# Attention operands written twice over into DRAM in full-width form, loads cut in pieces, bias copied per head

## The chip, the cores and the metric

The kernel runs on one core of a Trainium2 chip, as one program with one launch. The metric is the device time of that program in microseconds. All DMAs of the kernel are issued by SyncE (SP), on one queue that feeds the core's 16 DMA engines.

## The reference

One inference step of a hybrid decoder layer, in float32, for a prompt of 2048 tokens and 64 sample tokens (8 sequences of 8). The width is 1024; eight attention heads of 64 take one half of it and eight RWKV-7 heads of 64 the other.

```
def decoder_layer(x, k_past, v_past, wkv0, shift0, bias_table, ...):
    n = rms_norm(x, ln1_g)
    proj = n @ w_in                       # 1024 -> 1536 (q, k, v) + 1824 (RWKV)
    q = head_rms(q, q_norm_g);  k = head_rms(k, k_norm_g)
    att = dilated_attention(q, k_ctx, v_ctx, ...)
    rw, wkv_T, shift_T = rwkv7_time_mix(proj[..., 1536:], ...)
    h = x + concat(att, rw) @ w_out
    return h + square(relu(rms_norm(h, ln2_g) @ w_mlp1)) @ w_mlp2

# dilated_attention, for each (window, dilation) of (128, 1), (512, 4), (2048, 16):
s = einsum(q, k) * scale + bias[bucket(distance)];  e = exp(s - max);  o = e @ v
# the three branch outputs are merged, weighted by their denominators
```

The bias depends on head and distance alone: 32 buckets, 8 heads.

## The kernel before, in words

Float32 products are made from two-part operands: a tensor is split into a rounded high part and the rest, and each product is three matmuls (high x high, high x low, low x high).

The program has three stages. In the first (to about 1209 us) the projections run in four groups of 512 tokens (`proj`, `rproj`, `qkv`), and between their matmuls stand those of the RWKV recurrence, nine units one after the other (`core`). In the second (to about 1640 us) attention runs over four pairs of heads (`attention`), and the sample tokens' attention and the output projection follow. The third, from about 1960 us, is the MLP. The order of the instructions on each engine is laid down when the program is built, by a scheduler that plays a timeline; an instruction goes where its operands are ready in that timeline, by priority. On each engine the order is then fixed. Of the DMAs on SP the same holds: an issue that waits holds up all behind it. Eight semaphores serve the DMAs in turn, so that an issue also waits for the DMA eight places before it.

Weights come in panels of 256 KB (`wpanel`, L313): loaded to `wr`, of which there are two, then split by ACT and DVE into `wh` and `wl`, of which there are four each.

`qkv` makes q, k and v for a group. For q and k, `transposed_out` (L818) transposes two heads of a pair at a time, and writes a high part `qhi` and a low part `qlo` of 128 x 512 to DRAM (L831, L832), one DMA each, into `qhD`, `qlD`, `khD` and `klD`, which are laid out [pair, 128, 2048]. For k a third tile `ko` goes to an output. All of these, and others, share three buffers (tag `xg`). Group 0's q, k and v come last, after the last unit's projections.

`bias_vectors` (L458) makes, in group 1, the bias by distance for three branches (`bv1`, 8 heads x 1152), from one-hot tables `oh` by a matmul with the bias table (L468); it then copies `bv1` from DRAM to DRAM, 128 rows alike per head, into `bvD` (L477): two DMAs of four heads each. Seven more such one-hot pieces follow for the sample tokens. The generator is stepped once per `rproj` of group 1.

`attention(p)` needs for each of the pair's two heads three tiles of 128 x 2048: `kst` (high part of k in the upper and again in the lower 64 partitions), `klo` (the low part of k, twice) and `qst` (high part of q above, low part below). One matmul over 128 partitions then gives the sum of two products. `kq_load` (L994) loads them with twelve DMAs of 64 partitions, 512 KB each. Pair p+1's loads are written where branch 1 of pair p begins; two sets of tiles alternate, so pair 2's wait until pair 0 has ended. A pair takes 20 steps, in groups that each need a tile of V (`vt`, L1023, four buffers). While pair p+1 runs, the merge of pair p is stepped between its steps (`merge`): its weights go out to DRAM (`wD`, L1166), come back as rows (`wrow`, L1169), and a matmul spreads them over the partitions (`ax`, L1176).

Of the kernel before, what the change touches and what calls it, by code (L numbers as in the profile page):

```python
# [170 lines left out]
def _build(ctx, tc, nc, I, O, dbg, upto):  # L171
# [39 lines left out]
    qhD = dram.tile([4, P, T], F32, name="qhD")  # L211
    qlD = dram.tile([4, P, T], F32, name="qlD")
    khD = dram.tile([4, P, T], F32, name="khD")
    klD = dram.tile([4, P, T], F32, name="klD")
# [243 lines left out]
    def bias_vectors():  # L458

        btab = c1.tile([33, 8], F32, name="btab")  # L460
        nc.sync.dma_start(out=btab, in_=I["btab"])
        bv1 = dram.tile([8, 3, 384], F32, name="bv1")

        def by_distance(src, n):
            oh = wp.tile([P, 512], F32, name="oh", tag="qn", bufs=3)
            nc.sync.dma_start(out=oh[:33, :n], in_=src)
            ps = pj()
            PE.matmul(ps[:8, :n], btab, oh[:33, :n], start=True, stop=True)  # L468
            sb = wp.tile([P, 512], F32, name="sb", tag="qn", bufs=3)
            act(sb[:8, :n], ps[:8, :n], AF.Copy)  # L470
            return sb

        for b in range(3):
            nc.sync.dma_start(out=bv1[:, b], in_=by_distance(I["oneh"][:, b], 384)[:8, :384])
            yield
        for h in range(0, 8, 4):
            nc.sync.dma_start(out=bvD[h:h + 4].rearrange("h p b n -> h p (b n)"), in_=bc(bv1[h:h + 4].rearrange("h b n -> h (b n)"), 1, P))  # L477
        for c in range(0, NSV, 512):
            n = min(512, NSV - c)
            nc.sync.dma_start(out=svD[:, :, c:c + n], in_=bc(by_distance(I["soneh"][:, c:c + n], n)[:8, :n], 1, 8))  # L480
            yield
# [214 lines left out]
    def proj(g, nh, nl):  # L696

        other = qkv(g, nh, nl) if g else iter(())
        for i, j in enumerate((12, 13, 14, 4, 0, 8, 5, 1, 9, 6, 2, 10, 7, 3, 11)):
            rproj(g, j, nh, nl)  # L700
            if g == 1:
                next(bias, None)
# [68 lines left out]
    def qkv(g, nh, nl):  # L771
# [46 lines left out]
        def transposed_out(cp, qn):  # L818
            isq = cp < 2
            gg = gq if isq else gk  # L820
            hD, lD = (qhD, qlD) if isq else (khD, klD)
            h0 = (cp % 2) * 2
            for pp in range(2):
# [7 lines left out]
                nc.sync.dma_start(out=hD[h0 + pp, :, gs], in_=hi.bitcast(F32))  # L831
                nc.sync.dma_start(out=lD[h0 + pp, :, gs], in_=lo.bitcast(F32))  # L832
# [161 lines left out]
    def kq_load(p):  # L994

        kq = kqs[p % 2]
        K = []
        for ty in range(2):
            rr = slice(ty * 64, ty * 64 + 64)
            kst = kq.tile([P, T], F32R, name=f"kst{ty}", tag="kq")  # L1000
            klo = kq.tile([P, T], F32R, name=f"klo{ty}", tag="kq")
            qst = kq.tile([P, T], F32R, name=f"qst{ty}", tag="kq")
            for dst, src, r0 in ((kst, khD, 0), (qst, qhD, 0), (kst, khD, 64), (qst, qlD, 64), (klo, klD, 0), (klo, klD, 64)):
                nc.sync.dma_start(out=dst[r0:r0 + 64].bitcast(F32), in_=src[p, rr])
            K.append((kst, klo, qst))
        return K

# [29 lines left out]
    def attention(p, pump, ahead):  # L1037

        K = ahead.pop(("kq", p))
        st = at.tile([P, 2, 3, 4, 2, 4], F32, name="st", bufs=2)  # L1040
        ob = [at.tile([P, T], F32, name=f"ob{b}", bufs=2 if b == 0 else 1) for b in range(3)]
        for b in range(3):
            bts = ahead.pop(("bias", p, b))
            if p < 3:
                if b == 1:
                    ahead["kq", p + 1] = kq_load(p + 1)
                if b:
                    ahead["bias", p + 1, b - 1] = bias_load(p + 1, b - 1)
            vt = None
            for grp in range(4):  # L1050
                vp, vt = vt, next_v()
                o = ppo.tile([P, 512], F32, name="o")
                for t2 in range(0, 4, 2 if b < 2 else 4):
# [38 lines left out]
                    pump()  # L1092
                if b == 0:
# [3 lines left out]
                else:  # L1097
                    act(ob[b].rearrange("p (m r) -> p m r", r=16)[:, :, grp * 4:(grp + 1) * 4], o.rearrange("p (r m) -> p m r", r=4), AF.Copy)
        if p < 3:
# [83 lines left out]
    ahead = {("kq", 0): kq_load(0)}  # L1183
    for b in range(3):
        ahead["bias", 0, b] = bias_load(0, b)
    vq.append(next(vgen))
# [179 lines left out]
    for nm, t in (("mixR", mixR), ("mixA", mixA), ("qhD", qhD), ("qlD", qlD), ("khD", khD), ("klD", klD)):  # L1366
# [180 lines left out]
```

## Time and profile before

| | |
|---|---|
| median of 3 runs | 3410.0 us (3407.44 to 3411.9) |
| profiled execution, whole program | 3415.77 us |
| its span, first to last instruction | 3414.0 us |
| TensorE busy | 3209.2 us, 94% |
| VectorE, ScalarE, GpSimd busy | 50%, 39%, 12% |
| DMA | 364.73 MB, mean 107 GB/s |

Busy shares are averages over stages that have different limits, so the profile is read by stretch: which engine is busy there, and what the others wait for. PE is TensorE, DVE VectorE, ACT ScalarE, POOL GpSimd, and SPq the queue on which SyncE issues DMAs. The DMA share is the mean over the 16 DMA engines of the time in which they move packets, and GB/s is what they moved. A DMA's row on SPq shows its issue, not its transfer; a long one is an issue that was held up.

### The profile page before, as it was taken

The numbers are of one execution on the slowest core, as the hardware profiler recorded it, in microseconds if no ns is written. First come the engines' busy times: TensorE is split into PE (matmuls) and PEld (weight loads), VectorE is DVE, ScalarE is ACT, GpSimd is POOL, SyncE is SP. The second block draws the span as 40 slices with busy tenths as digits, with TensorE's granted clock in tenths as the row PEclk, the third lists the DMA queues.
The fourth block names the chain that finished last, engine by engine and source line by source line (L and its number), as shares of the span: only waits on it lengthen the run. The fifth ranks groups of instructions, "written<-read, shape, count | busy, mean of one in ns | idle before, by whom it ended". The sixth has DMA issues, their size and how long they took to land.

```text
span 3414.0 us, 60201 instructions
## 1 busy us (share of the span) xinstructions
PE 3209.2 (94%) x23646; PEld 2791.4 (82%) x23646; DVE 1713.4 (50%) x3951; ACT 1326.7 (39%) x3209; POOL 395.2 (12%) x713
## 2 busy tenths in 40 slices
PE   5959999999999979989899999999999999999999
PEld 5836877786788857878688899999999988888887
DVE  4635676677677525546554643333333633333333
ACT  4435564565455536657322322222222322222221
POOL 1003243342354100111000000000000000000000
PEclk9979999999999989999899999999999999999999
DMA  5445464465355495333776111111111211111112
GB/s 165 136 141 161 131 191 139 119 174 145 112 146 153 131 212 113 94 87 99 261 244 206 44 47 44 47 44 44 44 46 44 97 49 49 48 50 47 50 47 74
DMA packets 336968, 364.73 MB, mean 107 GB/s; under 512 B 112907, under 2 KB 226374, under 8 KB 333612
## 3 DMA queue, kind: packets, MB, share of 16 engines
q1 hardware_dynamic: 336684, 360.88, 36.5%
q8 instruction: 186, 3.05, 0.4%
q14 instruction: 98, 0.80, 0.1%
HBM read 286.20 MB, written 79.30 MB: 107 GB/s over the span
## 4 chain that ended last, share of the span: by engine, by line
PE 59%; DMA 6%; DVE 2%; SPq 1%; issue 1%; ACT 1%; POOL 1%; DVEq 0%; ACTq 0%; POOLq 0%
PE pm L1505 21%; PE pm L1488 21%; PE pwo L1431 4%; PE o L1091 2%; PE sc L1066 2%; PE pt L1084 2%; PE sc L1067 2%; PE pj L789 1%; DMA kst<-khD 1%; DMA vt<-vD 1%; DMA kv<-in_kc 1%; DMA mr<-mixA 1%; SPq L1421 1%; PE sc L1233 0%; DMA wD<-wh 0%
## 5 line engine op out<-in xcount | busy, mean ns | idle before, releaser
L184 ACT ACTIVATE wh<-wr 128x512 fp32r<-128x512 f32 (+1 forms) x472 | 294.3, 624 | 1027.5 <-PE pm L1505 582.3
L181 DVE TENSOR_TENSOR wl<-wr,wh 128x512 fp32r<-128x512 f32 (+1 forms) x472 | 325.9, 692 | 425.0 <-ACT wh L184 410.7
L1488 PE MATMUL pm<-mml,wh 128*128 128x512 f32 (+2 forms) x1280 | 452.5, 354 | 3.3 <-DVE mml L181 3.3
L1488 PE MATMUL pm<-mmh,wh 128*128 128x512 f32 (+2 forms) x1280 | 454.8, 356 | 0.4 <-ACT mmh L184 0.4
L1488 PE MATMUL pm<-mmh,wl 128*128 128x512 f32 (+2 forms) x1280 | 452.8, 354 | 0.0
L1505 PE MATMUL pm<-fh,wh 128*128 128x512 f32 (+2 forms) x1280 | 450.5, 355 | 0.0
L1505 PE MATMUL pm<-fh,wl 128*128 128x512 f32 (+2 forms) x1280 | 449.6, 353 | 0.0
L1505 PE MATMUL pm<-fl,wh 128*128 128x512 f32 (+2 forms) x1280 | 448.4, 352 | 0.0
L181 DVE TENSOR_TENSOR h<-pm,h 128x364 f32<-128x364 f32 (+1 forms) x320 | 190.5, 598 | 423.9 <-PE pm L1505 423.7
L1488 PEld LDWEIGHTS pm<-mml,wh 128*128 128x128 f32 x1280 | 241.0, 188 | 27.4 <-DVE mml L181 5.9
L1488 PEld LDWEIGHTS pm<-mmh,wl 128*128 128x128 f32 x1280 | 241.9, 189 | 22.5
L1505 PEld LDWEIGHTS pm<-fh,wl 128*128 128x128 f32 x1280 | 240.7, 188 | 22.4
L1488 PEld LDWEIGHTS pm<-mmh,wh 128*128 128x128 f32 x1280 | 241.4, 189 | 19.9 <-ACT mmh L184 0.9
L1505 PEld LDWEIGHTS pm<-fl,wh 128*128 128x128 f32 x1280 | 240.0, 188 | 21.5
L1505 PEld LDWEIGHTS pm<-fh,wh 128*128 128x128 f32 x1280 | 240.3, 188 | 19.2
L789 PE MATMUL pj<-wh,nh 128*128 128x256 f32 (+1 forms) x816 | 237.3, 292 | 7.5 <-ACT qn L184 3.5
L789 PE MATMUL pj<-wh,nl 128*128 128x256 f32 (+1 forms) x816 | 236.2, 290 | 1.0 <-DVE nl L181 0.9
L330 PE MATMUL pj<-nh,wh 128*128 128x512 f32 (+3 forms) x600 | 222.7, 375 | 13.2 <-ACT nh L184 9.9
L789 PE MATMUL pj<-wl,nh 128*128 128x256 f32 (+1 forms) x816 | 234.6, 288 | 0.0
L330 PE MATMUL pj<-nl,wh 128*128 128x512 f32 (+3 forms) x600 | 221.6, 370 | 3.9 <-DVE nl L181 3.8
L330 PE MATMUL pj<-nh,wl 128*128 128x512 f32 (+3 forms) x600 | 217.5, 365 | 0.0
L184 ACT ACTIVATE e<-e,st 128x256 f32<-128x256 f32 (+1 forms) x384 | 174.3, 455 | 106.3 <-DVE st L1069 104.4
(295 smaller groups left out, 6105.3 us busy)
## 6 DMA issues: line engine op xcount, KB each, us to landing
wr<-in_w SPq DMA_DIRECT2D x256, 256.0 KB
wr<-in_wr SPq DMA_DIRECT2D x120, 256.0 KB
wr<-in_wq SPq DMA_DIRECT2D x96, 256.0 KB
kv<-in_kc SPq DMA_DIRECT2D x40, 512.0 KB
kv<-in_vc SPq DMA_DIRECT2D x40, 512.0 KB
xsD<-xst SPq DMA_DIRECT2D x56, 256.0 KB
xrkv<-xsD SPq DMA_DIRECT2D x32, 384.0 KB
vt<-vD SPq DMA_DIRECT2D x48, 256.0 KB
```

The source lines that it names most:

```text
L181: V.tensor_tensor(out, a, b, op)
L184: S.activation(out, in_, func, bias=bias, scale=scale, **kw)
L330: PE.matmul(ps[:m, :n], a[:, k, :m], b[h * 4 + k][:, c0:c0 + n], start=(h == 0 and i == 0), stop=(h == 1 and i == 11))
L789: PE.matmul(out, a[h * 2 + k][:, i * P:i * P + m], b[:, k, :], start=(h == 0 and q == 0 and i % 2 == 0), stop=(h == 3 and q == 5 and (i % ...
L1066: PE.matmul(ps[:, c0:c0 + n], cols(qst, b, i, False), cols(kst, b, i, both), start=True, stop=False)
L1067: PE.matmul(ps[:, c0:c0 + n], cols(qst, b, i, False), cols(klo, b, i, both), start=False, stop=True)
L1084: PE.transpose(pt[:, y * P:(y + 1) * P], e[:, c0:c0 + P], ident)
L1091: PE.matmul(o[ty * 64:ty * 64 + 64, (i % 4) * P:(i % 4 + 1) * P], kv[:, ty * 64:ty * 64 + 64], ptss[ty][:, y * P:(y + 1) * P], start=fst, ...
L1421: nc.sync.dma_start(out=h[:, :, c0:c0 + NC_], in_=I["xh"][:, :, c0:c0 + NC_])
L1431: PE.matmul(ps[:, :NC_], a[k][:, o * P:(o + 1) * P], b, start=(i == 0), stop=(i == 3 * KT - 1))
L1488: PE.matmul(ps[:, :n], a[:, k], b[:, hf * 4 + k, c0:c0 + n], start=(hf == 0 and i == 0), stop=(hf == 1 and i == 11))
L1505: PE.matmul(ps[:, :n], a[:, f], b[:, c0:c0 + n], start=(i == 0), stop=(i == 11))
```

## The change

The four DRAM tensors become three: `qD`, `khD` and `klD`, laid out [pair, head of the pair, copy, 64, 2048], so that a head's tile of 128 partitions stands in DRAM as it will stand in the tile: the high part of k twice, the low part of k twice, and the high and low parts of q. `transposed_out` writes them with DMAs of 64 partitions x 512 columns (128 KB): four for each high and each low tile of k, two for each tile of q. `kq_load` loads 128 partitions at once and in pieces: for pair 0 four pieces of 512 columns for each of the six tiles, for the others two of 1024 columns. It hands back a generator, of which `attention` takes one piece after each step from branch 1 on. At the start of attention the two bias tiles of branch 0 and six pieces stand ahead of the first V tile. The bias is copied head by head, eight DMAs of 128 rows, and the generator of the bias is stepped through groups 1 and 2. In all SP issues 1666 DMAs where it issued 1520. In PE's order the first `ax` matmul of pair 0's merge stands behind the 131st of 384 score products, before and after.

```diff
--- before.py
+++ after.py
@@ -208,10 +208,10 @@
         return t
 
 
-    qhD = dram.tile([4, P, T], F32, name="qhD")
-    qlD = dram.tile([4, P, T], F32, name="qlD")
-    khD = dram.tile([4, P, T], F32, name="khD")
-    klD = dram.tile([4, P, T], F32, name="klD")
+
+    qD = dram.tile([4, 2, 2, 64, T], F32, name="qD")
+    khD = dram.tile([4, 2, 2, 64, T], F32, name="khD")
+    klD = dram.tile([4, 2, 2, 64, T], F32, name="klD")
     vD = dram.tile([T, 512], F32, name="vD")
     vSD = dram.tile([NS, 512], F32, name="vSD")
     qSD = dram.tile([4, P, NS], F32, name="qSD")
@@ -473,8 +473,9 @@
         for b in range(3):
             nc.sync.dma_start(out=bv1[:, b], in_=by_distance(I["oneh"][:, b], 384)[:8, :384])
             yield
-        for h in range(0, 8, 4):
-            nc.sync.dma_start(out=bvD[h:h + 4].rearrange("h p b n -> h p (b n)"), in_=bc(bv1[h:h + 4].rearrange("h b n -> h (b n)"), 1, P))
+        for h in range(8):
+            nc.sync.dma_start(out=bvD[h:h + 1].rearrange("h p b n -> h p (b n)"), in_=bc(bv1[h:h + 1].rearrange("h b n -> h (b n)"), 1, P))
+            yield
         for c in range(0, NSV, 512):
             n = min(512, NSV - c)
             nc.sync.dma_start(out=svD[:, :, c:c + n], in_=bc(by_distance(I["soneh"][:, c:c + n], n)[:8, :n], 1, 8))
@@ -698,7 +699,7 @@
         other = qkv(g, nh, nl) if g else iter(())
         for i, j in enumerate((12, 13, 14, 4, 0, 8, 5, 1, 9, 6, 2, 10, 7, 3, 11)):
             rproj(g, j, nh, nl)
-            if g == 1:
+            if g in (1, 2):
                 next(bias, None)
             if i in AFTER[g]:
                 next(other, None)
@@ -818,7 +819,7 @@
         def transposed_out(cp, qn):
             isq = cp < 2
             gg = gq if isq else gk
-            hD, lD = (qhD, qlD) if isq else (khD, klD)
+            hD, lD = (qD, qD) if isq else (khD, klD)
             h0 = (cp % 2) * 2
             for pp in range(2):
                 tp = pj()
@@ -828,8 +829,10 @@
                 act(hi, tp, AF.Copy, scale=gg)
                 lo = wp.tile([P, 512], F32R, name="qlo", tag="xg", bufs=3)
                 stt(lo, tp, gg, hi.bitcast(F32), ALU.mult, ALU.subtract)
-                nc.sync.dma_start(out=hD[h0 + pp, :, gs], in_=hi.bitcast(F32))
-                nc.sync.dma_start(out=lD[h0 + pp, :, gs], in_=lo.bitcast(F32))
+                for t, tD, xs in ((hi, hD, (0,) if isq else (0, 1)), (lo, lD, (1,) if isq else (0, 1))):
+                    for x in xs:
+                        for ty in range(2):
+                            nc.sync.dma_start(out=tD[h0 + pp, ty, x, :, gs], in_=t[64 * ty:64 * ty + 64].bitcast(F32))
                 if not isq:
                     ko = wp.tile([P, 512], F32, name="ko", tag="xg", bufs=3)
                     act(ko, tp, AF.Copy, scale=gg)
@@ -991,19 +994,20 @@
 
     evac.n = 0
 
-    def kq_load(p):
+    def kq_load(p, steps=2):
 
         kq = kqs[p % 2]
-        K = []
-        for ty in range(2):
-            rr = slice(ty * 64, ty * 64 + 64)
-            kst = kq.tile([P, T], F32R, name=f"kst{ty}", tag="kq")
-            klo = kq.tile([P, T], F32R, name=f"klo{ty}", tag="kq")
-            qst = kq.tile([P, T], F32R, name=f"qst{ty}", tag="kq")
-            for dst, src, r0 in ((kst, khD, 0), (qst, qhD, 0), (kst, khD, 64), (qst, qlD, 64), (klo, klD, 0), (klo, klD, 64)):
-                nc.sync.dma_start(out=dst[r0:r0 + 64].bitcast(F32), in_=src[p, rr])
-            K.append((kst, klo, qst))
-        return K
+        K = [[kq.tile([P, T], F32R, name=f"{nm}{ty}", tag="kq") for nm in ("kst", "klo", "qst")] for ty in range(2)]
+
+        def pieces():
+            for i in range(steps):
+                cs = slice(i * T // steps, (i + 1) * T // steps)
+                for ty in range(2):
+                    for dst, src in zip(K[ty], (khD, klD, qD)):
+                        nc.sync.dma_start(out=dst[:, cs].bitcast(F32), in_=src[p, ty].rearrange("x q t -> (x q) t")[:, cs])
+                        yield
+
+        return K, pieces()
 
     def bias_load(p, b):
         bts = []
@@ -1036,7 +1040,8 @@
 
     def attention(p, pump, ahead):
 
-        K = ahead.pop(("kq", p))
+        K, _ = ahead.pop(("kq", p))
+        coming = iter(())
         st = at.tile([P, 2, 3, 4, 2, 4], F32, name="st", bufs=2)
         ob = [at.tile([P, T], F32, name=f"ob{b}", bufs=2 if b == 0 else 1) for b in range(3)]
         for b in range(3):
@@ -1044,6 +1049,7 @@
             if p < 3:
                 if b == 1:
                     ahead["kq", p + 1] = kq_load(p + 1)
+                    coming = ahead["kq", p + 1][1]
                 if b:
                     ahead["bias", p + 1, b - 1] = bias_load(p + 1, b - 1)
             vt = None
@@ -1090,12 +1096,15 @@
                             i, kv, c0, fst, lst = work[ty][1][y]
                             PE.matmul(o[ty * 64:ty * 64 + 64, (i % 4) * P:(i % 4 + 1) * P], kv[:, ty * 64:ty * 64 + 64], ptss[ty][:, y * P:(y + 1) * P], start=fst, stop=lst, tile_position=(0, ty * 64))
                     pump()
+                    next(coming, None)
                 if b == 0:
                     act(ob[b][:, grp * 512:(grp + 1) * 512], o, AF.Copy)
                 elif b == 1:
                     act(ob[b][:, grp * 512:(grp + 1) * 512].rearrange("p (n q) -> p n q", q=4), o.rearrange("p (q n) -> p n q", q=4), AF.Copy)
                 else:
                     act(ob[b].rearrange("p (m r) -> p m r", r=16)[:, :, grp * 4:(grp + 1) * 4], o.rearrange("p (r m) -> p m r", r=4), AF.Copy)
+        for _ in coming:
+            pass
         if p < 3:
             ahead["bias", p + 1, 2] = bias_load(p + 1, 2)
         return merge(p, ob, st)
@@ -1180,10 +1189,13 @@
                 yield
             nc.sync.dma_start(out=mixA[p, :, cs], in_=ob[0][:, cs])
 
-    ahead = {("kq", 0): kq_load(0)}
-    for b in range(3):
+    ahead = {("bias", 0, 0): bias_load(0, 0)}
+    ahead["kq", 0] = kq_load(0, 4)
+    for i, _ in enumerate(ahead["kq", 0][1]):
+        if i == 5:
+            vq.append(next(vgen))
+    for b in range(1, 3):
         ahead["bias", 0, b] = bias_load(0, b)
-    vq.append(next(vgen))
     wsel = at.tile([P, 4, P], F32R, name="wsel")
     wsel0 = at.tile([P, 4, P], F32, name="wsel0", tag="pts", bufs=4)
     nc.sync.dma_start(out=wsel0, in_=I["wsel"])
...
```

On SP, at the bias copies (`bvD` is the copy's target, `wr` a weight panel, `xtd` and `tw` belong to the recurrence, `oh` is a one-hot table) before:

```order
L466 DMA oh<-in_soneh 33x512
L313 DMA wr<-in_wr 128x512
L477 DMA bvD<-bv_3887 512x1x1152 x2
L313 DMA wr<-in_wr 128x512
L466 DMA oh<-in_soneh 33x512
L346 DMA xsD<-xst 128x512
```

And after the change, at the same place on SP:

```order
L313 DMA wr<-in_wr 128x512 x2
L477 DMA bvD<-bv_3886 128x1x1152 x3
L346 DMA xsD<-xst 128x512
L313 DMA wr<-in_wr 128x512
L477 DMA bvD<-bv_3886 128x1x1152
L313 DMA wr<-in_wr 128x512
L574 DMA xtd<-xt 1024x1x32 x2
L477 DMA bvD<-bv_3886 128x1x1152 x4
L346 DMA xsD<-xst 128x512
L466 DMA oh<-in_soneh 33x512
L313 DMA wr<-in_wr 128x512
L576 DMA tw<-xtd 32x16x32 x4
```

The eight copies stand in three runs of three, one and four, and the sample tokens' first one-hot table has moved behind them; the PE matmul that uses it stands 192 projection matmuls later than before.

On SP, where the first stage ends and pair 0's tiles are loaded (`vD` is V in DRAM, `bt` a bias tile) before:

```order
L868 DMA out_o_vS<-qnS 64x256
L1004 DMA kst_14628<-khD 64x2048
L1004 DMA qst_14630<-qhD 64x2048
L1004 DMA kst_14628<-khD 64x2048
L1004 DMA qst_14630<-qlD 64x2048
L1004 DMA klo_14629<-klD 64x2048 x2
L1004 DMA kst_14637<-khD 64x2048
L871 DMA vD<-qn 128x2x256
```

And after the change, at the same place on SP:

```order
L1016 DMA bt_14761<-bvD 128x256
L1016 DMA bt_14763<-bvD 128x256
L1007 DMA kst_14765<-khD 128x512
L874 DMA vD<-qn 128x2x256
L875 DMA out_o_vwin<-qn 128x2x256
L1007 DMA klo_14766<-klD 128x512
L1007 DMA qst_14767<-qD 128x512
L313 DMA wr<-in_wq 128x512
L1007 DMA kst_14768<-khD 128x512
L1007 DMA klo_14769<-klD 128x512
L1007 DMA qst_14770<-qD 128x512
L313 DMA wr<-in_wq 128x512
```

The loads stood behind all stores of keys; now the first six pieces stand between the last weight panels, and the last key stores (pairs 2 and 3) and the other 18 pieces follow.

On SP, pair 1's loads during pair 0, after the change:

```order
L1027 DMA vt<-vD 128x4x128 x3
L1007 DMA kst_15170<-khD 128x1024
L1007 DMA klo_15171<-klD 128x1024
L1007 DMA qst_15172<-qD 128x1024
L1007 DMA kst_15173<-khD 128x1024
L1007 DMA klo_15174<-klD 128x1024
L1007 DMA qst_15175<-qD 128x1024
L1007 DMA kst_15170<-khD 128x1024
```

The 12 pieces (seven of them shown) stand in one run between the third and the next V tile, where the 12 loads stood before.

## Rows read from the trace of the kernel before

**Rows 1.** Stages: busy time of each engine, granted clock, DMA share, GB/s

```profile
195.00:245.00 50.00, 16.13 (x90) 9.60 (x88) 13.42 (x33) 10.16 (x27) 2.27 (x13) 0.68 0.34 123
245.00:1195.00 950.00, 902.04 (x8967) 739.33 (x8967) 636.12 (x1262) 533.06 (x1222) 322.19 (x579) 0.98 0.51 146
...
1960.00:3410.00 1450.00, 1449.76 (x7579) 1323.19 (x7577) 561.82 (x937) 332.47 (x585) 2.01 (x1) 1.00 0.17 51
```

**Rows 2.** Waits of PE, 0 to 250 us: total, times, longest

```profile
PE pj L468 <- DMA oh<-in_soneh: 27.5, 1, 27.5
```

**Rows 3.** Timeline of SP, 175 to 260 us: start, length, instruction, count

```profile
194.94 9.96 SPq L477 DMA_DIRECT2D bvD<-bv  x2
205.00 21.99 SPq L313 DMA_DIRECT2D wr<-in_wr  x1
227.04 0.37 SPq L466 DMA_DIRECT2D oh<-in_soneh  x1
```

**Rows 4.** Stretch during the bias copies

```profile
210.00:220.00 10.00, 2.96 (x34) 1.97 (x34) 4.62 (x12) 0.51 (x1) 0.12 (x1) 0.67 0.26 107
```

**Rows 5.** DMA issues of the whole program: count, size of each

```profile
bvD<-bv SPq DMA_DIRECT2D x2, 2304.0 KB
...
kst<-khD SPq DMA_DIRECT2D x16, 512.0 KB
```

**Rows 6.** Timeline of PE at the start of attention

```profile
1208.33 0.28 PE L789 MATMUL pj<-wh,nl 128*64 128x256 f32 x1
...
1230.90 0.58 PE L1066 MATMUL sc<-kst,qst 128*128 128x256 f32 x1 [0.17 <-DVE st L1069]
```

**Rows 7.** Waits of PE, 1195 to 1710 us

```profile
PE ax L1176 <- DMA wrow<-wD: 21.3, 2, 10.8
...
PE o L1091 <- DMA vt<-vD: 4.4, 1, 4.4
```

**Rows 8.** Stretches with loads over 64 partitions (first) and over 128

```profile
1240.00:1250.00 10.00, 10.00 (x93) 8.29 (x94) 6.37 (x29) 8.13 (x27) 0.00 (x0) 1.00 1.03 218
...
1695.00:1700.00 5.00, 5.00 (x44) 5.00 (x44) 2.86 (x6) 1.16 (x3) 0.00 (x0) 1.00 1.10 359
...
1720.00:1725.00 5.00, 5.00 (x53) 4.67 (x52) 2.10 (x11) 0.62 (x1) 0.00 (x0) 1.00 1.00 358
```

**Rows 9.** Timeline of SP: pair 2's loads and pair 0's merge

```profile
1326.93 0.48 SPq L1004 DMA_DIRECT2D kst<-khD  x1
...
1351.17 6.60 SPq L1166 DMA_DIRECT2D wD<-wh  x4
...
1365.30 0.61 SPq L1169 DMA_DIRECT2D wrow<-wD  x2
```

**Rows 10.** Timelines of DVE (first) and PE at the two merges

```profile
1347.43 0.55 DVE L181 TENSOR_TENSOR wh<-scw,wh 128x384 fp32r<-128x384 f32 x1
...
1368.09 0.76 PE L1176 MATMUL ax<-wrow,wsel 128*128 128x512 f32 x1 [10.49 <-DMA wrow<-wD]
...
1471.41 0.76 PE L1176 MATMUL ax<-wrow,wsel 128*128 128x512 f32 x1 [10.80 <-DMA wrow<-wD]
```

**Rows 11.** Stretch after the first merge's wait

```profile
1370.00:1380.00 10.00, 10.00 (x63) 7.84 (x59) 4.14 (x19) 5.11 (x19) 2.55 (x2) 0.83 0.18 52
```

**Rows 12.** Waits of SP and PE, 250 to 1195 us; waiters for khD, klD

```profile
SPq L313 <- DVE wl L181: 200.9, 103, 8.2
...
PE pj L840 <- ACT ko L184: 3.9, 1, 3.9
...
  ACT qhi L184: 4.0, 3
...
  DVE qlo L175: 4.2, 3
```

**Rows 13.** Timeline of SP: last weight panels and a key store

```profile
1187.11 0.95 SPq L313 DMA_DIRECT2D wr<-in_wq  x2
1188.15 0.38 SPq L831 DMA_DIRECT2D khD<-qhi  x1
```

More of the change, by code (lines that the diff above doesn't have):

```diff
@@ L1365, in _build @@
     ph2.close()
-    for nm, t in (("mixR", mixR), ("mixA", mixA), ("qhD", qhD), ("qlD", qlD), ("khD", khD), ("klD", klD)):
+    for nm, t in (("mixR", mixR), ("mixA", mixA)):
         if nm in dbg:
```

## The prediction

> **What bounds the kernel now.** I read the stages first. TensorE is busy for 1449.76 of 1450 us in the last stretch, the MLP, and for 902 of 950 us in the projections: there it is the bound, and the change touches none of its matmuls [rows 1]. So I looked for places where PE stands still for a DMA that the change touches. The reader should see four.
>
> The first lies in the stretch from 195 to 245 us, where PE is busy for 16 of 50 [rows 1]. It waits 27.5 us, once, for a one-hot table [rows 2]. The queue shows why: SP issues the two bias copies in 9.96 us, the next weight load then hangs 21.99 us in its issue, and only at 227.04 does the table's load go out [rows 3]. Meanwhile the 16 DMA engines are busy for 0.26 of the time and move 107 GB/s [rows 4]: about four engines work. Two copies of 2304 KB [rows 5] are 4.72 MB, which is 44 us at that rate, so they run from 195 to about 239.
>
> The second is the start of attention: the last projection matmul ends at 1208.6, and the matmuls flow again from 1230.90 [rows 6], when pair 0's 12 loads and the bias tiles behind them have landed. The third is 4.4 us for a V tile, the fourth 21.3 us in two waits for `wrow` [rows 7]. They have one cause: while `kst`, `klo` and `qst` arrive over 64 partitions, the engines are busy all the time (1.03) and yet move only 218 GB/s; loads over 128 partitions move 358 to 359 GB/s at a share of 1.00 to 1.10 [rows 8]. A pair's 6.29 MB takes 28.9 us at 218, and everything that SP issues behind it waits.
>
> **The change part by part**, against the profiled execution's 3415.8 us (span 3414.0; the median of the runs is 5.8 lower).
>
> *Bias copies.* Eight copies of 128 rows replace two whose outermost dimension is 4. The four busy engines fit that 4, so I take a copy over 128 rows to spread over all 16. Bounds for the 4.72 MB: 13 us at 359 GB/s, 44 us at 107 if nothing is gained. I take 13, because a transfer with 128 rows has the rate of the second kind of row. The order puts three copies, a weight load, one copy, a weight load, four copies on SP, and PE's next use of a one-hot table about 190 projection matmuls later. The longest block, 2.36 MB, holds the queue 6.6 us (22 at the slow rate); PE has up to four split panels of 12 matmuls ahead, near 0.2 us each by the MLP's row (7579 in 1449.76 us), so up to some 9 us. Residue: 0 to 17 us, taken as 2. What goes: at least the 27.5 us; at most 31.4, the 33.9 us of idle in 195 to 245 less the 2.5 that the projections show per 50 us [rows 1]. I take 29 - 2 = **27**. Late next are the weight panels behind the last four copies.
>
> *Start of attention.* SP now issues the first two bias tiles, six pieces (columns 0 to 511) and the first V tile before the last key stores; PE's first score matmuls wait for these pieces alone. Behind the last weight panel then stand 16 half stores (2.1 MB, 9.6 us at 218), 1.6 MB of others (4.4 us at 359) and six more pieces (4.4 us): 18.4 us. Before, the last panel was issued at 1187.1 [rows 13] and PE ended 21.5 us later, so columns 512 to 1023 are there in time. The other 12 pieces, the bias tiles, constants and three V tiles (4.8 MB) need 13.9 us more, until about 10.8 us after PE's last projection matmul. Pair 0 ended near 1326.9, where the first load into its tiles is issued [rows 9]; 96 us for 20 steps, so a group of two steps lasts 9.6 us, and group 1 waits 1 to 2 us for its V tile. Of the 22.3 us gap 2.4 held score matmuls that remain. Gain: 22.3 - 2.4 - 2 = **18**, bounds 5 (the rate stays 218) and 22.
>
> *Pair 1's loads and the V tile.* The 12 pieces don't stand between steps: nothing holds them, and SP has them back to back behind the V tiles, as it had the 12 loads. They take 17.5 us instead of 28.9, so the V tile behind them comes 11 us sooner: **4.4** goes, bounds 0 and 4.4.
>
> *Merge rows.* SP's order is as before here: the pieces, then `wD`, then `wrow`. Loads begin at 1326.93; `wD` was issued from 1351.17, `wrow` at 1365.30 [rows 9], though its input was done at 1347.98 [rows 10]. With the V and bias tiles between them 7.6 MB are 21 us at 359 GB/s: drained at 1348, `wD` on its way at once, and with some 2.3 us to land for each of the two, `wrow` is there by about 1355. PE came to it 10.49 us before 1368.09, at 1357.6. So 10.49 and, in the next pair, 10.80 us go [rows 10], with a margin of 2 to 3 us. After the stall the granted clock was 0.83 for ten fully busy microseconds, so in part the lower of its two levels [rows 11]: some 2 us each time, which go too. Gain **25**, bounds 8 and 25.
>
> *Stores.* Key tiles go out as four 64-partition stores instead of one store, query tiles as two: 128 more issues, and 8.4 MB more. An issue costs 0.38 us [rows 13], 49 us of SP in all. At 218 GB/s a half store takes 0.60 us: 32 key tiles x (2.4 - 0.73) and 32 query tiles x (1.2 - 0.73) are 68 us of DMA time; at 359 it would be 23. No row has such a store; I take 218, the row of the other 64-partition transfer. The queues were busy 0.51 of these 950 us [rows 1], so most hides behind matmuls. On the path: the three staging buffers are shared, and a tile is free only when its stores have landed. Before, that cost 4.0 and 4.2 us in six waits of ACT and DVE, and PE 3.9 us at the last tile [rows 12]. Now a tile is held 3 us longer (three more issues 1.2, half rate 1.7). Exposed as often as before (6 of 32 key tiles): 18 us of waits on ACT and DVE, of which PE feels about half, **-10**; at best 0, at worst all 32 in pairs, -48.
>
> The Trainium skill ("SBUF — State Buffer", "Can I just issue two DMAs to hit both halves?") says that two transfers, one to each half of the partitions, don't add up to a full-width one, since each reaches 8 of the 16 ports; that speaks against the new stores. By it the 68 us hold and the term is -10; without it, 23 us and about -5.
>
> Sum: 27 + 18 + 4 + 25 - 10 = 64. 3415.8 - 64 = 3352, and 5.8 lower for the median: **3346 us**.
>
> **Rivals.**
> 1. *The copies gain nothing*: sixteen engines read one 4.6 KB row over and over and together stay at 107 GB/s. For it: no row shows such a copy on 16 engines. Against: four engines did 27 GB/s each, as much as any row here gives per engine. The residue is 17 us and the clock's part remains: about 20 lost, 3366. Chance 0.13.
> 2. *The pieces are not faster* than 218 GB/s, though they span 128 partitions, because they are small or because they come in a block all the same; the change then doesn't do what it says. Start 5, V tile 0, merge 8 instead of 18, 4, 25: 34 lost, 3380. Against: a stretch with loads of 132 to 512 KB runs at 358 [rows 8]. Chance 0.09. The Trainium skill (same page, "The DMA setup-cost knee") gives each transfer some 2 us that don't shrink with size and wants large ones; taken one by one, 24 pieces would by my estimate need about 65 us. The row at 358 GB/s disagrees for queued transfers.
> 3. *Slower: the one queue becomes the bound of the projections.* SP issues stores and weight loads in order. If each of the 128 added issues delays the weight panels, and its DMA time too, the projections lengthen by 49 + 68 = 117 us against a gain of 74: 3453. It decides once more than 60% is exposed. Against: SP itself waits 200.9 us of that stage for panel buffers to come free [rows 12], so it has time to spare. Chance 0.05.
> 4. *More*: no residue anywhere, and the reordered projections fill part of their 48 us of idle: 31 + 22 + 4 + 25 and 10 more, 3318. Chance 0.08.
>
> **How the numbers follow.** Forecast 0.65. Range 3312 to 3392: it holds the forecast with its bounds and rivals 1, 2 and 4; the third and odd mixtures, about 0.1, are left out. What a measurement of this kernel can tell from no change is about 0.2%, 7 us, so 3403 to 3417 is "same". Faster: the forecast with rivals 1, 2 and 4, 0.95, less 0.03 for a queue that is exposed in part and so lands on "same": 0.92, 0.03, and slower 0.05.
>
> **What would show it.** Right: no PE wait of over 5 us for `oh`; DMA share near 1 while `bvD` is written; score matmuls within 3 us of the last projection matmul; some 350 GB/s while the pieces land; no `wrow` wait. Wrong: waits of PE for weight panels while key tiles are stored, SP rows of `bvD` or `khD` before late `wr` rows, or a stretch between 245 and the end of the projections in which PE is under 93% busy.

## The result, and the profile after

The changed kernel takes 3384.48 us (median of six runs, 3373.44 to 3393.78) against 3411.24: a ratio of 0.9918, 95% interval 0.9904 to 0.9932, or 27 us faster where 64 were forecast. It lies in the range, near its slow end. Below, a gain is (1 - ratio) x 3411 us, each kernel against the kernel before on the same chip, with its 95% interval in brackets; for the changed kernel that is 28 (23 to 33). The profiled execution is the fastest of the six (3373.44 us, span 3371.7), so its trace shows 42 us of gain where the median has 27.

The stretches that answer to [rows 1], in the changed kernel (busy time of PE, PEld, DVE, ACT and POOL, then granted clock, DMA share, GB/s):

```profile
195.00:245.00 50.00, 44.29 (x280) 33.27 (x280) 29.85 (x64) 27.01 (x65) 1.56 (x7) 0.93 0.72 210
245.00:1195.00 950.00, 886.21 (x8751) 722.87 (x8746) 614.83 (x1226) 516.55 (x1177) 320.70 (x578) 0.95 0.55 150
```

The stall at the bias is gone: PE is busy for 44 of 50 us instead of 16. But the long stretch behind it is worse than before: PE is less busy, and the clock 0.95 instead of 0.98. The queue where [rows 3] stood (SP, changed kernel):

```profile
193.09 1.82 SPq L477 DMA_DIRECT2D bvD<-bv  x3
...
202.87 5.37 SPq L477 DMA_DIRECT2D bvD<-bv  x4
...
209.01 0.41 SPq L466 DMA_DIRECT2D oh<-in_soneh  x1
```

The eight copies no longer hold the queue for long, and the table's load goes out 18 us earlier than in [rows 3]. At the start of attention (timeline of PE, changed kernel, against [rows 6]):

```profile
1211.59 0.28 PE L790 MATMUL pj<-wh,nl 128*64 128x256 f32 x1
1211.70 0.22 PE L1072 MATMUL sc<-kst,qst 128*128 128x128 f32 x1
```

The scores follow at once, but the last projection matmul ends 3 us later than before, though PE was some 28 us ahead at 245. The waits of PE from 1195 to 1710 us that answer to [rows 7], and the merge's rows on SP against [rows 9]:

```profile
PE sc L1072 <- DMA qst<-qD: 5.7, 3, 2.6
...
PE sc L1185 <- DMA wrow<-wD: 0.4, 1, 0.4
```

```profile
1331.67 1.33 SPq L1175 DMA_DIRECT2D wD<-wh  x4
...
1335.33 0.69 SPq L1178 DMA_DIRECT2D wrow<-wD  x2
```

`wD` is issued in 1.33 us instead of 6.60, and `wrow` 4 us after `wD` instead of 14. The rate while pieces land, to be read against [rows 8] (pair 0's, then two stretches of pair 2's):

```profile
1222.00:1227.00 5.00, 3.14 (x19) 2.39 (x18) 1.93 (x6) 1.17 (x4) 0.00 (x0) 0.50 0.90 311
...
1315.00:1320.00 5.00, 5.00 (x48) 3.83 (x40) 4.28 (x20) 4.12 (x15) 0.00 (x0) 1.00 0.98 348
...
1325.00:1330.00 5.00, 5.00 (x45) 4.05 (x44) 3.97 (x14) 4.65 (x17) 0.00 (x0) 1.00 1.04 401
```

Pair 2's pieces come as fast as forecast. Pair 0's come somewhat slower, at 311 GB/s, and PE waits 5.7 us for pieces of `qst`, which the forecast had not. The stores (DMA issues, count and size: one line of the kernel before, then two of the changed kernel):

```profile
khD<-qhi SPq DMA_DIRECT2D x16, 256.0 KB
...
khD<-qhi SPq DMA_DIRECT2D x64, 128.0 KB
...
qD<-qhi SPq DMA_DIRECT2D x32, 128.0 KB
```

So attention did nearly what was forecast and the projections did not. How far each profiled execution is ahead (-) or behind (+) the kernel before at five stations, in us from the first instruction, worked out from the traces. A trace is one execution: the changed kernel's and x6's are the fastest of their runs, e1's and e12's the slowest.

| kernel | 1201st projection matmul | last one | last score of pair 0 | of pair 2 | span |
|---|---|---|---|---|---|
| before (at) | 371.8 | 1208.6 | 1326.5 | 1535.9 | 3414.0 |
| changed | -19 | +3 | -16 | -43 | -42 |
| e1 bias alone | -18 | +7 | -21 | -22 | -23 |
| e2 all but bias | +2 | +26 | +10 | -14 | -14 |
| e5 no copy | -17 | -15 | -40 | -65 | -65 |
| e12 and 128 issues | -14 | +1 | -14 | -40 | -40 |
| x1 issues, same order | -17 | -16 | -44 | -67 | -65 |
| x6 bias, rows outside | -29 | -33 | -36 | -36 | -38 |
| x5 fastest | -30 | -34 | -47 | -73 | -69 |

### The profile page after: what moved, and what is told of

The parts are those of the page before. It is cut to its first block, busy times and chain, and to the rows that moved or that the text cites. A ratio compares the mean times of both kernels' runs of the same rounds, so it can differ in the third digit from the quotient of the medians.

```text
span 3371.7 us, 60353 instructions
## 1 busy us (share of the span) xinstructions
PE 3216.7 (95%) x23646; PEld 2797.7 (83%) x23646; DVE 1711.5 (51%) x3951; ACT 1329.8 (39%) x3209; POOL 394.2 (12%) x713
## 4 chain that ended last, share of the span: by engine, by line
PE 50%; DMA 1%; DVE 1%; issue 0%; ACT 0%; SPq 0%; DVEq 0%; ACTq 0%
PE pm L1517 22%; PE pm L1500 22%; PE pwo L1443 5%; DMA kv<-in_kc 1%; PE ax L1289 0%; PE sc L1245 0%; DMA mixA<-ob 0%; PE pt L1281 0%; DMA mr<-mixA 0%; DVE mml L181 0%; DVE mt L175 0%; DMA kv<-in_vc 0%; DMA wrow<-wD 0%; DMA wr<-in_w 0%; ACT pr L184 0%
## 5 line engine op out<-in xcount | busy, mean ns | idle before, releaser
L1443 PE MATMUL pwo<-mh,wo 128*128 128x264 f32 x1024 | 199.1, 291 | 2.9 <-DVE h L181 2.5
```

Of the source, the lines that this page charges most:

```text
L1443: PE.matmul(ps[:, :NC_], a[k][:, o * P:(o + 1) * P], b, start=(i == 0), stop=(i == 3 * KT - 1))
```

## The experiments

### One part at a time

The edits are shown shortened, from here on. e1: the kernel before with the eight copies.

```
+        for h in range(8):  # one copy each, then yield
-            if g == 1:
+            if g in (1, 2):
                 next(bias, None)
```

> The kernel before with the change to the bias copies alone (eight copies of one head, drawn in groups 1 and 2); layout, stores and loads as before. After the change the 27.5 us wait for oh was gone and yet the last projection matmul ended 3 us later than before. Theory 1, the stores: the gain of the copies is real, and the 128 added store issues took it back; here they are absent, so the projections end 25 to 30 us earlier and the time is 3381 to 3387 us. Theory 2, the copies' gain does not reach the end of the projections: the recurrence, which shares TensorE with them, gives it back in this kernel too, through short waits and a lower granted clock; the time is 3405 to 3413 us, and the stretch 245 to the last projection matmul shows more time at the lower clock than the kernel before.

3388.24 us, a gain of 20 (16 to 25). Neither theory's: the gain is there, but the station table shows it elsewhere than expected. The last projection matmul is 7 us late, and the scores then need not wait. PE's waits from 1165 to 1240 us in e1:

```profile
PE pj L790 <- ACT wh L184: 10.1, 1, 10.1
PE pj L827 <- ACT qn L184: 6.5, 1, 6.5
```

SP had issued pair 0's key loads from 1168.56 on, ahead of the last weight panels at 1186.59; what attention gained at its start, the projections lost at their end. But 11 of the 25 us that the projections lost behind the first station were gone by the 2601st matmul, at 777 us, well before any key load: from 245 us to the end of the projections PE stood idle for 69 us (48 before) and had the clock's lower level, 1.2 GHz, for 79 (36 before). To that extent theory 2 holds.

e2: the changed kernel with the two old copies.

> The changed kernel with the bias copies as they were (two copies of four heads, drawn in group 1): layout, split stores and pieces remain. The wait of 27 us for oh is back. Theory 1, the stores: they cost about 30 us in the projections, the attention gains 42 to 45, so the last projection matmul ends near 1240 us and the time is 3393 to 3400 us. Theory 2: the stores cost little (0 to 10 us), the last projection matmul ends within 10 us of 1208.6 and the time is 3365 to 3378 us, as fast as the whole change or faster.

3399.21 us, a gain of 12 (8 to 16): theory 1, and the last projection matmul 26 us late. The stores, or something that comes with them, cost the projections some 25 us.

### The stores

e3 and e5 store as before, without a second copy; a load reads its 128 rows from two lots of 64. e4 keeps the copies, but one store covers 128 partitions.

```
# e3: two lots outside
+ ap=[[0 if keys else P * T, 2], [T, 64], [1, n]]
# e4: scratch laid out [4, 2, 64, 2, T], rows of the two lots interleaved
+ nc.sync.dma_start(out=dst, in_=bc(t.bitcast(F32), 1, 2))   # keys; queries: dst[:, x]
# e5: 64 rows outside
+ ap=[[T, 64], [0 if keys else P * T, 2], [1, n]]
```

> The changed kernel with the scratch layout and the stores of before (one store of 128 partitions per tile, no second copy, 128 issues and 8.4 MB fewer), while the loads still fill 128 partitions with one DMA each: the source of a load is read as two lots of 64 rows, for the keys the same 64 rows twice. Theory 1, the stores: the projections get back what they took, the last projection matmul ends near 1182 us, and the time is 3350 to 3360 us. Theory 2: the last projection matmul stays within 8 us of 1212 us and the time is 3370 to 3385 us. Either way the score matmuls follow the last projection matmul at once and the waits for wrow stay under 1 us, unless the source in two lots is read more slowly than one run of 128 rows.

3754.87 us, 346 slower, so it says nothing on the stores. The stretch shows why (e3, while key loads run):

```profile
1180.00:1190.00 10.00, 5.56 (x24) 4.97 (x25) 2.04 (x3) 3.64 (x7) 0.00 (x0) 0.50 0.13 50
```

A DMA share of 0.13 is two of 16 engines, as the two lots outside; the old bias copies, with four outside, stood at 0.26 [rows 4].

> The changed kernel with rows interleaved in the scratch tensors, so that every store covers 128 partitions with one DMA: the 8.4 MB of the keys' second copy are still written, but the store issues are as many as before. Between the run without a second copy and the changed kernel: under theory 1, if the 128 issues on the one queue cost, 3350 to 3360 us as without the copy; if the bytes cost, 3375 to 3385 us. Under theory 2 all three are alike within 10 us.

3364.84 us, a gain of 46 (41 to 51): 18 more than the changed kernel with the same bytes and 128 issues fewer. That is between theory 1's two ranges, so that issues and bytes both seemed to cost.

> As the run without narrow stores (one store of 128 partitions per tile, no second copy of the keys), but each load reads its source as 64 rows with two lots inside each, so that rows are interleaved in the operand tiles. In the earlier form, two lots outside and 64 rows inside, the DMA share stood at 0.13 and 50 GB/s while such loads ran. Theory 1: the number of lots outside decides over how many DMA engines a transfer is spread; with 64 outside the loads land at 300 to 360 GB/s again and the time is 3345 to 3365 us, the run with wide stores (3364.84 us) less what the 8.4 MB of second copies cost. Rival: the step of zero (the same 64 rows twice) is what is slow; then the key loads stay near 50 GB/s and the time is above 3600 us.

3352.22 us, a gain of 62 (57 to 67). Theory 1: with 64 rows outside the loads run at full rate, here pair 0's in e5, and the step of zero is not what was slow:

```profile
1180.00:1185.00 5.00, 4.71 (x37) 4.50 (x36) 0.69 (x1) 1.22 (x2) 0.00 (x0) 0.92 1.06 376
```

The second copies cost another 16, the stores 34 in all.

### The loads of the next pair

e7 is e4, e11 is e5, with six whole loads issued at once; e8 is e1 with the twelve loads of 64 partitions one between each two steps.

```
# e7, e11
-                    coming = ahead["kq", p + 1][1]
+                    ahead["kq", p + 1] = kq_load(p + 1, 1)   # all drawn here
```

> The kernel with wide stores, with the next pair's six tiles each loaded by one DMA of 128 partitions, all issued together at the start of the second part as before, not in pieces between steps. Theory 1, the pieces: the small transfers of the merge (wD, wrow) again queue behind 6 MB of key loads, the waits for wrow come back, 10 us in each of two pairs, and the time is 3380 to 3390 us. Theory 2, the width: at 358 GB/s the six loads are through in 18 us, before the merge needs the queue, and the time is 3362 to 3370 us.

> The kernel before with the bias change (3388.24 us alone), and the next pair's twelve loads of 64 partitions issued one between each two steps, layout and stores as before. Theory 1, the pieces: the spread alone frees the merges, 20 to 26 us, and the time is 3362 to 3370 us, as fast as the kernel with wide stores. Theory 2, the width: twelve loads at 218 GB/s still keep the engines busy over the merges and the time is 3380 to 3390 us.

> The kernel without second copies, with the next pair's six tiles loaded whole and all issued at once. With wide stores that made no difference (3364.44 against 3364.84 us): at 128 partitions the loads are through before the merge needs the queue. The same here: 3348 to 3357 us. If the pieces matter once the stores are light, it is above 3360 us.

e7 3364.44 us (gain 53, 45 to 60), e11 3347.79 (64, 59 to 68), no slower than with pieces; e8 3388.95 (25, 20 to 29), hardly more than e1. PE's waits from 1195 to 1710 us in e8:

```profile
PE ax L1188 <- DMA wrow<-wD: 22.4, 2, 11.5
```

The waits for `wrow` are there in full; e7 and e11 have none. So the width frees the merges, and whole loads do as well as halves. What e8 was meant to show of spreading it can't: on SP its twelve loads still leave in one run, from 1300.3 to 1319.2 us for pair 2, as before and as the pieces of the changed kernel do. No run spreads the loads over the steps.

### The bias copies in other settings

e6 is e4, and e9 is e5, with the old copies; e10 is e5 without any, and its bias is then not the reference's.

```
# e10
-    in_=bass.AP(tensor=bvD.tensor, ..., ap=[[1151, P], [1, 256]])
+    in_=bass.AP(tensor=bv1.tensor, ..., ap=[[1, P], [1, 256]])
```

> The kernel with wide stores (3364.84 us), with the bias copies of before. It prices the bias change a third time: 3408.6 to 3388.24 us alone, 3399.21 to 3384.48 us in the changed kernel, that is 15 to 20 us and not the 27 us forecast. Theory 1: the projections give back some 10 us of the 27 whatever stands around them; then 3380 to 3386 us. Rival: what it is worth depends on the order in which the queue then issues (loads of keys before or behind the last weight panels); then it can be anything from 0 to 27 us, 3365 to 3392 us, and a time below 3376 us or above 3388 us speaks for it.

> The kernel without second copies (3352.22 us) with the bias copies of before. With split stores the bias change was worth 14.7 us, with wide stores 2.8 us, alone 20.4 us. Theory 1: the wait for oh that it takes away is lost again in the projections, in short waits and at the lower granted clock, so that it is worth 0 to 12 us: 3352 to 3364 us. Rival: in a kernel whose queue is less loaded the 27 us come through: 3372 us or more.

> The kernel without second copies (3352.22 us), with the bias vectors not copied to 128 rows at all: the tiles of the bias are read from the short table itself, with a step of one value per partition, so that the bias is not the reference's. Removes eight transfers of 576 KB from the projections' start and leaves the wait for oh away too. Theory 1, the head start of 27 us is lost whatever the copies cost: 3340 to 3354 us. Rival, the eight copies themselves take back what the removed wait gives, by their load on the DMA engines: 3325 to 3338 us.

e6 3367.59 us (gain 46, 40 to 52): the bias change is worth nothing there. e9 3376.32 us (gain 35, 30 to 40): worth 27 there, its rival. e10 3340.71 us (gain 72, 67 to 76), 10 more than e5, within theory 1. One edit, priced 20, 16, 0 and 27: something else moved with it. The second copies have no fixed price either: with the old bias copies the kernel that writes them is the faster one (e6 46, e9 35), with the new ones the slower (e4 46, e5 62).

### Issues or order

What moves is the order on TensorE. The recurrence transposes its results in 18 blocks of four (`cs<-ident,yc`), and each kernel's order has a number of projection matmuls ahead of each block. Ahead of the 12th of them (the expectations call it the 45th, counting single transposes from zero):

| before, e9, x5, x6 | e10 | e6 | e5 (e1, e3, e4, e7, e8, e11) | x1 | e12 | changed | e2 | x3 | x4 | x2 |
|---|---|---|---|---|---|---|---|---|---|---|
| 3006 | 2949 | 2942 | 2891 | 2894 | 2687 | 2704 | 2718 | 2742 | 2976 | 3036 |

e12 adds 128 stores of one value, read from the tile stored. x1 copies them from the stored rows, at the lowest priority. x3 has two buffers of tag `xg`; x2 (from e5) and x4 (from the changed kernel) give the recurrence less of a head start.

```
# e12: + nc.sync.dma_start(out=tiny[n:n + 1], in_=t[0:1, 0:1])
# x1:  + tc.cur_priority += 1 << 22
#      + nc.sync.dma_start(out=tiny[n:n + 1], in_=dst[0:1, gs.start:gs.start + 1])
# x3:  - tag="xg", bufs=3      + tag="xg", bufs=2
# x2, x4: - FILL = 1 << 20     + FILL = 1000
```

> The kernel without second copies, with 128 stores of one value each added behind the stores of the key and query tiles, as many as the split stores add, each read from the tile stored. Between the changed kernel (3384.48 us) and wide stores (3364.84 us) lie 19.6 us for these issues at equal bytes. Theory 1, the issue itself: the one queue spends 0.4 to 0.6 us on each, what is queued behind comes later, and the time is 3365 to 3375 us. Theory 2, the width: a transfer of 64 partitions keeps its tile longer, and the issues cost nothing; 3350 to 3358 us.

> The kernel without second copies (3352.22 us) with 128 stores of one value added on the same queue, now copied from the scratch tensor just written and given the lowest priority, so that the recurrence's steps on TensorE stand where they do without them (the 45th block of transposes behind 2894 projection matmuls, 2891 without; 2687 in the run whose 128 issues changed the order, 3371.43 us). Theory 1, the issues cost on the chip: 3365 to 3375 us. Theory 2, the order costs: 3350 to 3357 us.

> The kernel without second copies (3352.22 us) with two buffers instead of three for the tiles that hold the hi and lo parts and the squares. No issue is added, but the scheduler then writes nearly the order of the kernel with 128 more issues (the 25th block behind 1941 projection matmuls, 1998 before, 1923 there; the 45th behind 2742, 2891 before, 2687 there). Theory 2, the order costs: 3365 to 3375 us. Theory 1: the issues cost, so here 3350 to 3357 us, unless the missing buffer itself costs, which would show as waits of ScalarE and VectorE for stores of these tiles.

> The kernel without second copies (3352.22 us) with a smaller head start in priority for the recurrence, so that from the middle on its steps stand later among the projections (the 45th block behind 3036 projection matmuls instead of 2891, the 55th behind 3432 instead of 3288, the last two behind all 4248). Theory 2, the order costs: it is not the same, and if a recurrence that runs ahead is what costs, a later one gains, up to the point where its end comes last: 3335 to 3350 us, or above 3360 us where the tail of the recurrence is then left over behind the projections. Theory 1: within 4 us of 3352 us.

> The changed kernel (3384.48 us), split stores and all, with the smaller head start for the recurrence (the 45th block behind 2976 projection matmuls instead of 2704, the 55th behind 3391 instead of 3144). Theory 2, the order costs: 3362 to 3374 us, near the kernel with wide stores. Theory 1: 3380 to 3388 us, since the 128 issues are all still there.

e12 3371.43 us (gain 41, 35 to 46): 128 issues without bytes cost 21. x1 3350.42 us (gain 65, 60 to 69): as many issues on the same queue cost nothing when the order stays nearly as it was; 105 of them go out before the last projection matmul, 23 behind it. So SP's time is not it, and in e12 SP even waits longer than in x1 for panel buffers to come free (261 and 229 us from 245 us to the last projection matmul). Nor are held tiles: ACT and DVE wait 24 us for stores of these tiles in e12, 33 in x1 and 35 in e5 (summed from the waits of 245 to 1195 us). What is left is the order; its effect shows in the time of the 12th block (timelines of PE: e5, then e12):

```profile
881.36 0.60 PE L612 MATMUL cs<-ident,yc 128*128 128x128 f32 x4
```

```profile
843.95 0.60 PE L613 MATMUL cs<-ident,yc 128*128 128x128 f32 x4
```

In e12 the recurrence is 37 us further and the projections, at their 2601st matmul, 42 us behind; the changed kernel has the same picture (838.95, and 30 behind e5). The end of the projections then comes 16 us later. Summed from the traces between 245 us and that end, against x1: 14 of e12's 18 us are more busy time of PE, with the clock at 1.2 GHz for 85 us instead of 51, and 3 are idle time. Why PE loses its full clock for longer in that order is open.

x3 3387.85 us, 38 slower than e5, fits the order but has the missing buffer in it (ACT and DVE wait 42 us for stores there). x2 3408.51 us (55 slower than e5) and x4 3427.94 (41 slower than the changed kernel) change a priority alone, and so show that order by itself can cost this much; but a later recurrence lost instead of gaining, and in a way of its own. Its end is left over behind the projections, so that the first scores come 36 us after them in x2 and 28 in x4. In x2:

```profile
1201.00:1237.00 36.00, 11.62 (x200) 8.37 (x200) 11.96 (x24) 4.63 (x11) 5.49 (x4) 0.58 0.69 234
```

e12 has no such tail. So neither earlier nor later is better as such, theory 2's forecast for x4 was wrong, and that e12's order costs 21 us rests on x1 and on what it leaves out: no run has that order without the issues.

### The bias with nothing moved

x6 is the kernel before with one line changed, and every instruction in its place; x5 is e11 with that line.

```
-        ... out=bvD[h:h + 4].rearrange("h p b n -> h p (b n)"), in_=bc(..., 1, P))
+        ... out=bvD[h:h + 4].rearrange("h p b n -> p h (b n)"), in_=bc(..., 0, P))
```

> The kernel before with the two bias copies written with the 128 rows as the outermost dimension instead of the four heads; every instruction on every engine stands where it stood. If a transfer is spread over as many DMA engines as its outermost dimension allows, the copies take 13 us or little more, the wait of 27.5 us for oh goes, and since the order is the same nothing is given back: theory 1, the time is 25 to 31 us shorter than before, 3378 to 3389 us. Rival, the projections lose part of any head start again, whatever the order: 5 to 20 us shorter.

> The fastest version (no second copies, loads at once, 3347.79 us) with those two copies in place of the eight, and so with the order of the kernel before on TensorE in the projections. The run without second copies and with the old copies, in that order, took 3376.32 us with the wait of 27 us in it. Theory 1: without it 3346 to 3352 us, as fast as the fastest version, the old order being no worse than the new one. Rival, the old order is the worse one and the change gained from the new one: above 3356 us.

x6 3385.3 us, a gain of 29 (24 to 33), and the station table has it whole, 33 in that execution, at the end of the projections. Theory 1. The copies (x6, against [rows 4]):

```profile
200.00:205.00 5.00, 5.00 (x22) 3.48 (x20) 0.84 (x2) 1.21 (x3) 0.00 (x0) 0.93 1.02 290
205.00:210.00 5.00, 1.54 (x7) 0.60 (x6) 4.44 (x12) 4.75 (x14) 0.12 (x1) 1.00 1.08 346
```

x5 3345.99 us, a gain of 66 (61 to 71): with e11 and x1 the fastest of the versions that keep the reference's bias, 38 us faster than the changed kernel and 1.9% faster than before.

## Why the prediction was off

**Bias copies, 27.** Right in mechanism and size: 29 when nothing else moves (x6), 27 in e9 and e5. All 16 engines took part (a DMA share of 1.03 and 380 GB/s from 200 to 205 us in the changed kernel), and PE's wait for `oh` fell from 27.5 to 1.1 us, so the first rival is out. In the change as it is, it brought 16 (e2).

**Start of attention, 18, and V tile, 4.4.** The profiled execution went from 3 us behind to 16 ahead there: 20 of 22. It is 25 in e5, 15 in e9 and 13 in x5. (The step's 4.8 MB at 359 GB/s are 13.4 us and not 13.9, which changes nothing.)

**Merge rows, 25.** From 16 ahead to 43: 27. Right, and by the width, so the second rival is out: whole loads over 128 partitions do as well as pieces (e7, e11), loads over 64 do not (e8).

**Stores, -10: this step failed.** The stores cost 34 us. The step reckoned with tiles held longer, 18 us of waits on ACT and DVE, of which PE feels half. Waits of ACT and DVE for stores of these tiles did grow, from 21 to 33 us (query tiles and `ko` counted, which the 8 us of the step leave out), but e5 has 35, and PE's waits for those tiles fell from 7 to 3. The longest of each in the changed kernel, 245 to 1195 us, against [rows 12]:

```profile
ACT qsq L184 <- DMA qD<-qlo: 12.9, 7, 2.8
```

```profile
PE pj L843 <- ACT ko L184: 2.1, 1, 2.1
```

What the step left out is that the order on TensorE is itself made from a timeline in which the issues stand: with 128 more of them the recurrence's steps moved forward past some 300 projection matmuls against before (190 against e5). I had compared the orders only at the bias, at the start of attention and at pair 1's loads, and took the projections' length from the trace of the old order. About 18 to 24 us of the 34 go with the order (e4 against the changed kernel, e12 against x1). That is shown by leaving other causes out, and not fully: e4 also stores over 128 partitions, and no run has the split stores in e5's order. The other 10 to 16 come with the second copies; e4 has nearly e5's order and the same waits for stores (32 us), so where they arise is open. With the old bias copies, in other orders, the stores cost 23 in all (e9 against e2). The runs of kernels with copies scatter (e7 3350 to 3368 us, e11 3345 to 3351).

In the changed kernel's own trace the loss reads so. From 245 us to the end of the projections PE was busy for only 13 us less than before (903 against 916), though 99 fewer of its projection matmuls were left, and it stood idle for 16 us more (64 against 48): 3 us later. The clock was at 1.2 GHz for 96 us of that stretch; before for 36, in e5 for 55. One such place (the changed kernel, then e5):

```profile
490.00:500.00 10.00, 7.91 (x89) 4.15 (x89) 9.84 (x20) 4.98 (x11) 8.98 (x15) 0.69 0.68 201
500.00:510.00 10.00, 8.85 (x61) 6.16 (x61) 8.21 (x15) 3.51 (x8) 8.59 (x19) 0.50 0.63 167
```

```profile
490.00:500.00 10.00, 10.00 (x84) 6.93 (x82) 9.74 (x18) 6.51 (x16) 8.67 (x18) 1.00 0.46 144
500.00:510.00 10.00, 10.00 (x81) 5.10 (x80) 9.57 (x19) 6.11 (x14) 6.99 (x12) 1.00 0.24 53
```

Before it, PE of the changed kernel had stood for 4.0 us, to 478, and twice for 0.9 us, to 489 and 493, for operands of the recurrence, and ran at 1.2 GHz from 494 to 511. In x5 the long stretch has the clock of before again and more work done than the changed kernel's:

```profile
245.00:1195.00 950.00, 897.04 (x8978) 739.52 (x8977) 628.97 (x1271) 525.71 (x1217) 322.20 (x578) 0.98 0.53 152
```

**The sum.** With the parts added one after the other: the loads alone gain 35 (e9), where the terms for attention were 47; the bias copies bring 27 more (e5: 62), as forecast; the stores take 34 of it (the changed kernel: 28). So of the 36 that are missing from the 64, the stores' term makes 24 and attention's terms 12, some 8 of them at its start.

**The third rival** asked for a late queue that keeps weight panels from PE. x1 denies it: 105 issues more within the projections, no time. In the changed kernel, too, SP had time to spare (245 to 1195 us, against the first of [rows 12]):

```profile
SPq L313 <- DVE wl L181: 210.0, 84, 13.1
```

PE waited there for a split panel once, for 2.2 us. The rival's sign, PE under 93% busy from 245 us on, was nearly met (886 of 950 us, 93.3%) for another reason.

## What to carry to other kernels

Where a scheduler lays down the order, a change of DMAs can change the order on every engine: compare the whole order, not only the edited places, and price a part by an edit that moves nothing (x6) or with the order held (x1). Write the dimension with the most rows outermost in a DMA, on both sides. A second copy in DRAM isn't needed for a load over 128 partitions, since the source of a load may name the same rows twice.

## What the runs showed of the hardware

By the DMA share, a transfer ran on about as many of the 16 engines as the smaller of its two outermost dimensions, at source and at target: two (0.13, 50 GB/s, e3), four (0.26, 107 GB/s, [rows 4]), all of them where it was 64 (1.06, 376 GB/s, e5) or 128 (1.08, 346 GB/s, x6). The Trainium skill ("DMA: Bandwidth & Descriptors", "Rules for kernel authors") says that an outermost dimension of size c, below 16, confines a DMA to at most c engines; the traces agree. The same section says that transfers under 64 KB are mostly overhead; 128 of four bytes each, 105 of them in a stretch where the DMA share was 0.52, cost no time that the runs can tell (x1 3350.42 us, e5 3352.22).
